# A two-layer DiT trunk on one core: the Fourier stage without GpSimd, x's squares summed by TensorE, fixed orders

## The chip, the cores and the metric

The kernel runs on one core of a Trainium2 chip. A core has five engines with instruction queues of their own: TensorE (PE, matmuls, with its weight loads as PEld), VectorE (DVE), ScalarE (ACT), GpSimd (POOL) and SyncE (SP, which issues most DMAs). The metric is the device time of one execution in microseconds.

## The reference, cut to what matters

Two layers over 512 tokens of width 1024. Layer 0 mixes by attention, layer 1 by a Fourier transform; each ends with a gated ConvFFN. The part that the change touches runs from the end of layer 0 to the start of layer 1's FFN:

```python
# end of layer 0
x = x + g2 * rms_norm(conv_ffn(h, ...), norm_g[0, 3])
# layer 1
h = modulate(rms_norm(x, norm_g[1, 0]), sh1, sc1)
y = fourier_mix(h) @ w_f                 # fft2 over (tokens, 256 channels of each of 4 groups), real part
x = x + g1 * rms_norm(y, norm_g[1, 1])
h = modulate(rms_norm(x, norm_g[1, 2]), sh2, sc2)
x = x + g2 * rms_norm(conv_ffn(h, ...), norm_g[1, 3])

def rms_norm(x, g):
    return x * lax.rsqrt(jnp.mean(x * x, axis=-1, keepdims=True) + EPS) * g
```

## The kernel before, in words

**Layout.** Activations are kept transposed: `xT` and `yT` are 128 partitions x 8 channel tiles x 512 tokens, in fp32. The tokens are worked in two halves of 256 (`halves`), so that one half's norms and updates run beside the other half's matmuls. Every matmul of size is done as three (`mm3`, lines 107 to 111), on a high and a low part of each operand. A high part is a cast on ACT, a low part a subtraction on DVE; `split` (line 130) issues both.

**What sets the order.** The program is written in one order, and a planner then places each engine's instructions by priority and by its own costs. `later(n)` shifts the priority (a negative number is earlier), `follow(i, j)` and `behind_pe` write an order between two instructions of one engine by hand, and `fence`/`held` keep some DVE and ACT work behind a point of the program. Parts that are to be interleaved are generators, advanced by `pump`.

**Norms.** The sum over channels is a matmul with ones: `stat_add` (line 195) adds a tile of squares in four matmuls with 32 output rows; `rstd` takes the reciprocal root (one ACT, four DVE operations); `spread` (line 227) brings the result to all partitions with one more matmul and copies it to SBUF as `Rs`. `YStat` squares y as its tiles are finished, adds most squares on POOL (line 303) and gives the last ones to PE directly.

**The last down sweep of layer 0** (`down_part`, `part`) makes y tile by tile, first for half 0, then for half 1. After half 0, `between` issues the update of x for half 0, `plain.tiles`, so that it runs beside half 1's matmuls: for each of eight tiles a DVE product of y, the gate `der` and `Rs`, a DVE add into `xT`, a high part `hst` on ACT and a low part `lst` on DVE of x times the layer's scale, a square on ACT, and an add of six of the eight squares on POOL (line 421) into `yT`'s tile 0.

**The Fourier stage.** `over_channels(g, h)` transforms the channels of group g for the two token tiles of half h into `Z` (half 0 scaled by its rms factor on the way out of PSUM; for half 1 the factor goes into the token tables, `tables(1, r1)`). `group(g, ts)` then sums over the token tiles `ts` with the cosine tables `ct` into `A` and with the sine tables `st` into `B`; `cosines(None, ...)` makes the Nyquist rows `N`. The rms factors are wanted with tokens on partitions, which `columns` (line 462) makes: four matmuls with the squares as stationary operand, and `rstd` on four columns. `shift` makes the transform of the constant shift. Half 1's update of x (`rest`) is pumped in between. The products with the weights (`wh`, `wl` of `w_f`) follow.

**Passages.** `joined` is the step from attention to layer 0's FFN: update of x, squares, sums, factor, and `remod`, which makes the FFN's operands `hh`, `hl` two tiles at a time or, for the tiles in `single`, one at a time. `joint` is the same step from the Fourier stage to layer 1's FFN, with two tiles per DVE product (`both` broadcasts the factor); its sums are advanced by `plain.runs`.

Of the kernel before, what the change touches and what calls it, by code (L numbers as in the profile page):

```python
# [85 lines left out]
def kernel(ctx: ExitStack, tc: tile.TileContext, a):  # L86
# [29 lines left out]


# [246 lines left out]
    def joined(ys, h, pps, nxt):  # L364
# [37 lines left out]
    class Plain:  # L402

        def __init__(self):
            self.acc = yT[:, 0, :]
            self.last = yT[:, KC - 1, :]

        def tiles(self, ys, h, l, gi, pps, am, eng=None):
            hs = halves[h]
            R = stat_bcast(ys.sums(pps, h), pps)  # L410
            yield
            for k in range(KC):
                x_update(h, l, gi, R, k, eng)
                x = xT[:, k, hs]
                S.activation(out=hst[:, k, hs], in_=x, func=AF.Copy, scale=am[:, k:k + 1])
                V.scalar_tensor_tensor(out=lst[:, k, hs], in0=x, scalar=am[:, k:k + 1], in1=f(hst[:, k, hs]),  # L416
                                       op0=ALU.mult, op1=ALU.subtract)
                sq = mk(cp, [P, T], F32, "sq", 2)[:, :HT] if 0 < k < KC - 1 else (self.last if k else self.acc)[:, hs]
                S.activation(out=sq, in_=x, func=AF.Square)
                if 0 < k < KC - 1:  # L420
                    G.tensor_tensor(out=self.acc[:, hs], in0=self.acc[:, hs], in1=sq, op=ALU.add)
                if k % 2:
                    yield


        def joint(self, ys, h, pps, am):
# [13 lines left out]
            for ks in ([[0], [1]] if h == 0 else [[0, 1]]) + [[2, 3], [4, 5], [6, 7]]:  # L440
# [3 lines left out]
                with later(0 if h else -10000):  # L444
                    V.tensor_tensor(out=t, in0=y, in1=both(R, n), op=ALU.mult)
                    i = V.tensor_tensor(out=x, in0=x, in1=t, op=ALU.add)
                    if h == 0 and ks == [1]:
                        self.mark = i
                    for k in ks:
                        S.activation(out=hh[:, k, hs], in_=xT[:, k, hs], func=AF.Copy, scale=am[:, k:k + 1])  # L450
                        V.scalar_tensor_tensor(out=hl[:, k, hs], in0=xT[:, k, hs], scalar=am[:, k:k + 1],
                                               in1=f(hh[:, k, hs]), op0=ALU.mult, op1=ALU.subtract)
                if ks[-1] % 2:
                    y = yT[:, ks[-1] - 1:ks[-1] + 1, hs]
                    S.activation(out=y, in_=xT[:, ks[-1] - 1:ks[-1] + 1, hs], func=AF.Square)
# [6 lines left out]
        def columns(self, h, pps):  # L462
            ps = mk(pps, [P, T], F32, "misc", 2)
            for i in range(2):
                t = 2 * h + i
                for n, s in enumerate((self.acc, self.last)):
                    PE.matmul(ps[:, 2 * i:2 * i + 2], lhsT=s[:, t * P:(t + 1) * P], rhs=ones32[:, :2], start=n == 0,
                              stop=n == 1)
            return rstd(ps[:, :4])
# [903 lines left out]
    def ffn(l, xp, ready, pre, mid, gem, plain=None):  # L1373
# [43 lines left out]
        def down_part(gi, w, g_, d, hs, ps=None, end=False):  # L1417
# [5 lines left out]
            if end:  # L1423
                ys.add(pps, yT[:, d, sl], hs)

# [116 lines left out]
        for gi, (f0, nch) in enumerate(GROUPS[l]):  # L1542
# [78 lines left out]
    def between(y):  # L1621
        fourier_early(2)
        pump(plain.tiles(y, 0, 0, 3, pps, n1[0], V), 6)
# [10 lines left out]
    with ExitStack() as es:  # L1634
# [15 lines left out]
        split(ft[0], ft[1], raw([P, 2, 256], a["dft_c"]), G)  # L1650
# [4 lines left out]
        def over_channels(g, h):  # L1655
            ps = mk(pps, [P, 2, 256], F32, *(("misc", 2) if h else ("mm", 6)))
            m = {}
            for i in range(2):
                ts_ = slice((2 * h + i) * P, (2 * h + i + 1) * P)
                for c in range(2):  # L1660
                    k = 2 * g + c
                    m[i, c] = mm3(ps[:, i, :], hst[:, k, ts_], lst[:, k, ts_], ft[0][:, c, :], ft[1][:, c, :],
                                  i + c == 0, i + c == 2)

            for c in range(2):
                follow(m[1, c][c], m[0, c][c])
# [3 lines left out]
            for t in range(2):  # L1670
                rc = r0[:, 2 * t:2 * t + 1]
                held(S.activation(out=Z[0][:, t, g, :], in_=ps[:, t, :], func=AF.Copy, scale=rc))
                held(V.scalar_tensor_tensor(out=Z[1][:, t, g, :], in0=ps[:, t, :], scalar=rc,
                                            in1=f(Z[0][:, t, g, :]), op0=ALU.mult, op1=ALU.subtract))


        def tables(h, r=None):
            if h == 0:
                for (th, tl), src in ((ct, lc), (st, ls)):
                    split(th[:, 0:2, :], tl[:, 0:2, :], src[:, 0:2, :], G)  # L1680
                return
            for i in range(2):
                t = 2 * h + i
                rc = r[:, 2 * i:2 * i + 1]
                for (th, tl), src in ((ct, lc), (st, ls)):
                    S.activation(out=th[:, t, :], in_=src[:, t, :], func=AF.Copy, scale=rc)
                    V.scalar_tensor_tensor(out=tl[:, t, :], in0=src[:, t, :], scalar=rc, in1=f(th[:, t, :]),
# [35 lines left out]
        def cosines(key, dst, lhs, ts, b):  # L1723
            ps = over_tokens(key, 0, lhs, ct, ts)
            if ts[-1] == TT - 1:
# [200 lines left out]
```

## Time and profile before

| | |
|---|---|
| runs of the kernel | 1110.02, 1112.4, 1114.91 us; median 1112.4 us |
| profiled execution | 1111.27 us, of which the span from first to last instruction is 1109.5 us |
| mean granted TensorE clock | 0.995 |
| busy: PE, DVE, ACT, POOL | 1082.2, 896.1, 595.7, 128.9 us |

Times in the profile count from the start of the span. A row of the timeline has the start, the duration, the engine, the line, the operation with output <- inputs, and the shapes; a bracket tells how long the engine was idle before it and who ended that. Neighbouring instructions of one kind are merged (xN). A plain fp32 matmul (the sums, the spread) leaves two records, each of the three of `mm3` one. A row of the stretches has the length and then, for each engine, the busy time and the number of instructions, the granted TensorE clock (1.00 is full speed), the DMA share and GB/s. A row of the waits has who waited for whom, the total in us, how often, and the longest. A row of the groups has the number of instructions, the busy us in all and the mean in ns.

### The profile page before, as it was taken

How to read it: one execution, taken by the hardware profiler on the slowest of the kernel's cores; microseconds unless marked ns; L12 is line 12 of the kernel's file. 1: busy time of each engine (PE TensorE's matmuls, PEld its weight loads, DVE VectorE, ACT ScalarE, POOL GpSimd, SP SyncE). 2: the span in 40 equal slices, each digit the busy share in tenths (PEclk: the TensorE clock that was granted, in tenths of full speed). 3: DMA queues.
4: the chain of work that ended last, by engine and by line, in shares of the span. 5: the costliest groups of instructions: out<-in, count | busy, mean ns of one | idle time of the engine just before them, and what ended most of it. 6: DMA issues, size and time to landing. Idle time of an engine off the chain costs nothing. (4 is left out here: it accounts for less than half of the span.)

```text
span 1109.5 us, 22276 instructions
## 1 busy us (share of the span) xinstructions
PE 1082.2 (98%) x9220; PEld 1013.0 (91%) x9220; DVE 896.1 (81%) x1457; ACT 595.7 (54%) x1047; POOL 128.9 (12%) x136
## 2 busy tenths in 40 slices
PE   9999999999999999999999998999999999999995
PEld 5699888869899999999999998989999999999995
DVE  5789877664689966879999878878997998979756
ACT  4452455665666633552465446768755654655542
POOL 0046123412100000000000133300000000000012
PEclk9999999999999999999999999999999999999998
DMA  9676100273231565327624600833206433332342
GB/s 368 273 256 209 39 18 22 76 292 126 77 153 42 173 242 204 115 86 263 245 77 164 232 35 21 281 100 134 77 30 196 147 109 115 105 105 86 105 148 77
DMA packets 33774, 156.01 MB, mean 141 GB/s; under 512 B 3460, under 2 KB 8196, under 8 KB 22024
## 3 DMA queue, kind: packets, MB, share of 16 engines
q1 hardware_dynamic: 32520, 150.39, 37.9%
q0 software_dynamic: 1152, 4.19, 1.5%
q8 instruction: 72, 1.18, 0.4%
q14 instruction: 30, 0.25, 0.1%
HBM read 148.28 MB, written 6.29 MB: 139 GB/s over the span
## 5 line engine op out<-in xcount | busy, mean ns | idle before, releaser
L131 ACT CAST wh<-raw 128x1024 fp32r<-128x1024 f32 (+2 forms) x207 | 190.7, 933 | 145.5 <-PE mm L109 102.0
L131 DVE TENSOR_TENSOR wl<-raw,wh 128x1024 fp32r<-128x1024 f32 (+2 forms) x205 | 219.9, 1079 | 60.4 <-ACT wh L131 57.8
L108 PE MATMUL mm<-hh,wh 128*128 128x256 f32 x856 | 240.7, 283 | 3.6 <-ACT sq L1335 1.9
L109 PE MATMUL mm<-hl,wh 128*128 128x256 f32 x856 | 238.0, 279 | 0.4 <-DVE hl L353 0.3
L110 PE MATMUL mm<-hh,wl 128*128 128x256 f32 x856 | 237.7, 278 | 0.5 <-DVE wl L131 0.5
L108 PEld LDWEIGHTS mm<-hh,wh 128*128 128x128 f32 x856 | 161.0, 189 | 9.8 <-ACT sq L1335 6.1
L109 PEld LDWEIGHTS mm<-hl,wh 128*128 128x128 f32 x856 | 161.2, 188 | 0.9 <-DVE hl L353 0.5
L110 PEld LDWEIGHTS mm<-hh,wl 128*128 128x128 f32 x856 | 160.8, 188 | 0.7 <-DVE wl L131 0.7
L108 PE MATMUL mm<-xh,wh 128*128 128x256 f32 x492 | 136.8, 279 | 0.0
L109 PE MATMUL mm<-xl,wh 128*128 128x256 f32 x492 | 136.7, 278 | 0.0
L110 PE MATMUL mm<-xh,wl 128*128 128x256 f32 x492 | 136.5, 278 | 0.0
L108 PE MATMUL mm<-zh,wh 128*128 128x256 f32 x384 | 109.4, 285 | 0.3
L109 PE MATMUL mm<-zl,wh 128*128 128x256 f32 x384 | 106.3, 277 | 0.0
L110 PE MATMUL mm<-zh,wl 128*128 128x256 f32 x384 | 106.3, 277 | 0.0
L108 PEld LDWEIGHTS mm<-xh,wh 128*128 128x128 f32 x492 | 92.3, 188 | 1.2 <-issue 0.8
L109 PEld LDWEIGHTS mm<-xl,wh 128*128 128x128 f32 x492 | 92.5, 188 | 0.6 <-issue 0.4
L110 PEld LDWEIGHTS mm<-xh,wl 128*128 128x128 f32 x492 | 92.5, 188 | 0.1
L108 PEld LDWEIGHTS mm<-zh,wh 128*128 128x128 f32 x384 | 72.1, 188 | 5.5 <-ACT sq L1338 4.7
L109 PEld LDWEIGHTS mm<-zl,wh 128*128 128x128 f32 x384 | 72.2, 188 | 0.0
L110 PEld LDWEIGHTS mm<-zh,wl 128*128 128x128 f32 x384 | 72.1, 188 | 0.0
L303 POOL TENSOR_TENSOR gacc<-gacc,sq 128x256 f32<-128x256 f32 (+1 forms) x23 | 20.4, 887 | 396.6 <-ACT sq L301 396.2
L1396 ACT ACTIVATE cv<-mm,cols 128x512 f32<-128x512 f32 x59 | 45.8, 779 | 12.1 <-PE mm L110 8.2
(457 smaller groups left out, 2794.8 us busy)
## 6 DMA issues: line engine op xcount, KB each, us to landing
raw<-in_w_up SPq DMA_DIRECT2D x42, 1024.0 KB, 4.9
xT<-in_mod_r SPq DMA_DIRECT2D x20, 1024.0 KB, 5.0
raw<-in_w_down SPq DMA_DIRECT2D x32, 384.0 KB, 3.1
raw<-in_mod_p SPq DMA_DIRECT2D x8, 1024.0 KB, 5.1
raw<-in_w_down SPq DMA_DIRECT2D x16, 512.0 KB, 4.5
raw<-in_w_in SPq DMA_DIRECT2D x6, 1024.0 KB, 8.0
yT<-in_mod_r SPq DMA_DIRECT2D x10, 512.0 KB, 6.8
raw<-in_w_out SPq DMA_DIRECT2D x4, 1024.0 KB, 5.8
```

The lines of the kernel that those rows point to most:

```text
L108: i = PE.matmul(out, lhsT=ah, rhs=bh, start=start, stop=False, skip_group_check=skip)
L109: PE.matmul(out, lhsT=ah, rhs=bl, start=False, stop=False, skip_group_check=skip)
L110: return i, PE.matmul(out, lhsT=al, rhs=bh, start=False, stop=stop, skip_group_check=skip)
L131: i = S.copy(out=h, in_=src), eng.tensor_tensor(out=l, in0=src, in1=f(h), op=ALU.subtract)
L303: G.tensor_tensor(out=self.acc[:, sl], in0=self.acc[:, sl], in1=sq[:, sl], op=ALU.add)
L1396: S.activation(out=cv, in_=ps, func=AF.Identity, bias=bc, scale=wc[1])
```

## The change

- `Plain.tiles` becomes `Plain.gated`. The gate is multiplied into y in the down sweep (one ACT operation per part); the update is done on pairs of tiles, product and add on DVE; the squares are written over y in pairs, and nothing is added on POOL. For half 1 the product of the first pair reads the factor from PSUM, and the DVE operations have a written order.
- `Plain.totals` sums all eight tiles of squares on PE with `stat_add` and takes `rstd`; `columns` then turns the result with two small matmuls and a copy. For half 0 both stand in the last down sweep (`first_norms`, behind the parts of tiles 6 and 7).
- The splits of `ft` and of the tables of half 0 move from POOL to DVE.
- PE's order in the Fourier stage is written out with `in_turn`: each matmul follows the one before it in the program. `shift` comes late, token tiles 2 and 3 are summed in two rounds over the groups, and the Nyquist sums come last.
- `joint` gets a written DVE order for half 0 and other priorities; `joined` makes the first two tiles of half 0 one at a time; `md(pair=True)` drops leftover half buffers.

The diff, cut to its core:

```diff
+    def in_turn(step, *args):
+        ops = nc.cur_bb.bb.instructions
+        at = len(ops)
+        r = step(*args)
+        for o in [o for o in ops[at:] if o.engine == mybir.EngineType.PE]:
+            if turn[0] is not None:
+                tc.add_manual_dep(o, turn[0], ...)
+            turn[0] = o.name
+        return r
...
     def md(pair=False):
-        if pair or not spare_md:
+        if pair:
+            spare_md.clear()
+        if not spare_md:
...
         for k in range(0, KC, 2):
             with later(-10000 if h else 0):
-                remod(h, *nxt, R, [k], (0, 4) if h else ())
+                remod(h, *nxt, R, [k], (0, 4) if h else (0,))
...
-        def tiles(self, ys, h, l, gi, pps, am, eng=None):
+        def gated(self, ys, h, pps, am):
             hs = halves[h]
-            R = stat_bcast(ys.sums(pps, h), pps)
+            r = rstd(ys.sums(pps, h)[:, :W4])
             yield
+            if h:
+                Rp, Rs = spread(r, pps, copy=False)
+                R = mk(cp, [P, HT], F32, "Rs", 3)
+                S.copy(out=R, in_=Rp)
+            else:
+                Rp = R = spread(r, pps)
+            yield
+            turn, low = [], []
+            for k in range(0, KC, 2):
+                x, y = (v[:, k:k + 2, hs] for v in (xT, yT))
+                t = md(True)
+                with later(-10000 if h else 0):
+                    turn.append(V.tensor_tensor(out=t, in0=y, in1=both(R if k else Rp), op=ALU.mult))
+                    turn.append(V.tensor_tensor(out=x, in0=x, in1=t, op=ALU.add))
+                    for c in (k, k + 1):
+                        S.activation(out=hst[:, c, hs], in_=xT[:, c, hs], func=AF.Copy, scale=am[:, c:c + 1])
+                        low.append(V.scalar_tensor_tensor(out=lst[:, c, hs], in0=xT[:, c, hs], ...))
+                    S.activation(out=y, in_=x, func=AF.Square)
+            if h:
+                turn = turn[:2] + low[:2] + turn[2:] + low[2:]
+                for n in range(1, len(turn)):
+                    follow(turn[n], turn[n - 1])
+
+        def totals(self, h, pps):
+            ps = mk(pps, [P, T], F32, "misc", 2)
             for k in range(KC):
...
-                if 0 < k < KC - 1:
-                    G.tensor_tensor(out=self.acc[:, hs], in0=self.acc[:, hs], in1=sq, op=ALU.add)
+                stat_add(ps, yT[:, k, halves[h]], HT, k == 0, k == KC - 1)
+            with later(-10000):
+                return rstd(ps[:, :W4])
...
         def joint(self, ys, h, pps, am):
...
+                    i = [update(ks) for ks in ([0], [1], [2, 3], [4, 5], [6, 7])]
+                turn = [*i[0], *i[1], line[0], line[1], *i[2]]
+                for n in (3, 4):
+                    turn += [line[2 * n - 4], line[2 * n - 3], *i[n]]
+                for n in range(1, len(turn)):
+                    follow(turn[n], turn[n - 1])
+                self.mark = i[2][1]
...
-        def columns(self, h, pps):
+        def columns(self, h, r, pps):
             ps = mk(pps, [P, T], F32, "misc", 2)
-            for i in range(2):
-                t = 2 * h + i
-                for n, s in enumerate((self.acc, self.last)):
-                    PE.matmul(ps[:, 2 * i:2 * i + 2], lhsT=s[:, t * P:(t + 1) * P], rhs=ones32[:, :2], ...)
-            return rstd(ps[:, :4])
+            for b in range(2):
+                PE.matmul(ps[64 * b:64 * b + 64, :2], lhsT=r, rhs=con[:, K_QD + b:K_QD + 4:2], start=True, stop=True)
+            c = mk(fx, [P, 2], F32, "rc%d" % h)
+            with later(-10000):
+                V.tensor_copy(out=c, in_=ps[:, :2])
+            return c
...
             if end:
                 ys.add(pps, yT[:, d, sl], hs)
+                if l == 0:
+                    S.activation(out=yT[:, d, sl], in_=yT[:, d, sl], func=AF.Copy, scale=der[:, 0, 3, d:d + 1])
...
                 for d in range(1, KC):
                     part(d, [1])
+                    if l == 0 and d > KC - 3:
+                        behind_pe(norms)
...
-        split(ft[0], ft[1], raw([P, 2, 256], a["dft_c"]), G)
+        split(ft[0], ft[1], raw([P, 2, 256], a["dft_c"]))
...
-            ps = mk(pps, [P, 2, 256], F32, *(("misc", 2) if h else ("mm", 6)))
+            ps = mk(pps, [P, 2, 256], F32, *(("misc", 2) if h and g != 2 else ("mm", 6)))
...
-                    split(th[:, 0:2, :], tl[:, 0:2, :], src[:, 0:2, :], G)
+                    split(th[:, 0:2, :], tl[:, 0:2, :], src[:, 0:2, :])
...
-        r0 = plain.columns(0, pps)
-        fb = shift()
+        fences.clear()
         tables(0)
-        nyh, nyl = wpair([4, D])
-        split(nyh, nyl, raw([4, D], a["w_ny"]))
-        rest = plain.tiles(ys, 1, 0, 3, pps, n1[0], V)
-        pump(rest)
-        over_channels(0, 0)
-        fence()
-        over_channels(3, 0)
-        pump(rest)
...
+        rest = plain.gated(ys, 1, pps, n1[0])
+        in_turn(over_channels, 0, 0)
+        in_turn(pump, rest)
+        for g in (1, 2):
+            in_turn(over_channels, g, 0)
+        in_turn(pump, rest)
+        pump(rest)
+        in_turn(over_channels, 3, 0)
+        in_turn(group, 0, [0, 1])
+        in_turn(over_channels, 0, 1)
+        for g in (1, 2):
+            in_turn(group, g, [0, 1])
+        v1 = in_turn(plain.totals, 1, pps)
+        for g in (1, 2):
+            in_turn(over_channels, g, 1)
+        nyh, nyl = wpair([4, D])
+        split(nyh, nyl, raw([4, D], a["w_ny"]))
+        r1 = in_turn(plain.columns, 1, v1, pps)
+        tables(1, r1)
+        in_turn(over_channels, 3, 1)
+        in_turn(group, 3, [0, 1])
+        fb = in_turn(shift)
+        for g in (2, 0, 1, 3):
+            in_turn(group, g, [2])
         fence()
+        for g in (2, 0, 1, 3):
+            in_turn(group, g, [3])
+        in_turn(cosines, None, N, [z[:, :, :, P] for z in Z], list(range(TT)), True)
```

More of the change, by code (lines that the diff above doesn't have):

```diff
@@ L115, in follow @@
             mybir.DependencyClass.NoSync, mybir.DependencyReason.DATA), reason="order")
+    turn = [None]
+    def in_turn(step, *args):
[4 more added lines that the diff above has]
+            if turn[0] is not None:
+                tc.add_manual_dep(o, turn[0], mybir.DependencyInfo(
+                    mybir.DependencyClass.NoSync, mybir.DependencyReason.DATA), reason="order")
+            turn[0] = o.name
+        return r
     fences = {}
@@ L439, in joint, with update @@
             yield
-            for ks in ([[0], [1]] if h == 0 else [[0, 1]]) + [[2, 3], [4, 5], [6, 7]]:
+            line = {}
+            def update(ks):
                 n = len(ks)
@@ L443, in joint @@
                 t = md(True)[:, :n, :]
[L444 to L452, printed above, removed]
+                i = V.tensor_tensor(out=t, in0=y, in1=both(R, n), op=ALU.mult)
+                j = V.tensor_tensor(out=x, in0=x, in1=t, op=ALU.add)
+                for k in ks:
+                    S.activation(out=hh[:, k, hs], in_=xT[:, k, hs], func=AF.Copy, scale=am[:, k:k + 1])
+                    line[k] = V.scalar_tensor_tensor(out=hl[:, k, hs], in0=xT[:, k, hs], scalar=am[:, k:k + 1],
+                                                     in1=f(hh[:, k, hs]), op0=ALU.mult, op1=ALU.subtract)
                 if ks[-1] % 2:
                     y = yT[:, ks[-1] - 1:ks[-1] + 1, hs]
-                    S.activation(out=y, in_=xT[:, ks[-1] - 1:ks[-1] + 1, hs], func=AF.Square)
+                    with later(0 if h else 10000):
+                        S.activation(out=y, in_=xT[:, ks[-1] - 1:ks[-1] + 1, hs], func=AF.Square)
+                return i, j
+            if h:
+                for k in range(0, KC, 2):
+                    update([k, k + 1])
+            else:
+                with later(-10000):
[6 more added lines that the diff above has]
+                self.mark = i[2][1]
             yield
@@ L1622, in between, with first_norms @@
         fourier_early(2)
-        pump(plain.tiles(y, 0, 0, 3, pps, n1[0], V), 6)
+        pump(plain.gated(y, 0, pps, n1[0]), 10)
+    def first_norms():
+        r = plain.totals(0, pps)
+        yield
+        rc.append(plain.columns(0, r, pps))
+    rc = []
+    norms = first_norms()
     with ExitStack() as es:
@@ L1661, in over_channels @@
                     k = 2 * g + c
[L1662 to L1666, printed above, removed]
+                    mm3(ps[:, i, :], hst[:, k, ts_], lst[:, k, ts_], ft[0][:, c, :], ft[1][:, c, :],
+                        i + c == 0, i + c == 2)
             if h:
@@ L1670, in over_channels @@
             for t in range(2):
[L1671 to L1674, printed above, removed]
+                r = rc[0][:, t:t + 1]
+                S.activation(out=Z[0][:, t, g, :], in_=ps[:, t, :], func=AF.Copy, scale=r)
+                V.scalar_tensor_tensor(out=Z[1][:, t, g, :], in0=ps[:, t, :], scalar=r,
+                                       in1=f(Z[0][:, t, g, :]), op0=ALU.mult, op1=ALU.subtract)
         def tables(h, r=None):
```

49 lines of the change are left out of this document (9 added, 40 removed).

## The prediction

> **What bounds the kernel now.** I read the page first, then the busy time by stretches around the Fourier stage, the waits of the whole run, and the timelines of that stage.
>
> ```profile
> span 1109.5 us, 22276 instructions
> ...
> PE 1082.2 (98%) x9220; PEld 1013.0 (91%) x9220; DVE 896.1 (81%) x1457; ACT 595.7 (54%) x1047; POOL 128.9 (12%) x136
> ```
>
> TensorE (PE) is busy for 1082.2 of 1109.5 us. Anything that takes work from another engine pays only where PE waits for that engine. So the size of the prize is the time that PE loses in the stage that is edited:
>
> ```profile
> core 0: us, PE busy (x) PEld busy (x) DVE busy (x) ACT busy (x) POOL busy (x), PEclk, DMA share, GB/s
> 651.70:665.90 14.20, 14.20 (x122) 14.20 (x121) 14.17 (x26) 7.60 (x20) 8.82 (x9) 1.00 0.01 2
> 665.90:676.70 10.80, 10.23 (x104) 9.57 (x103) 8.43 (x24) 6.54 (x17) 3.97 (x5) 0.84 0.17 51
> 676.70:692.70 16.00, 13.73 (x106) 12.56 (x104) 14.39 (x34) 9.56 (x25) 5.54 (x6) 1.00 0.01 2
> ```
>
> From 651.70 to 665.90 the last down sweep runs on PE without a gap, although VectorE (DVE) is full (14.17 of 14.20): what the first half's update costs there is hidden. From 665.90 on PE has gaps (13.73 of 16.00) and once a lowered clock (0.84). The waits say for whom:
>
> ```profile
> PE misc L467 <- POOL yT L421: 1.2, 1, 1.2
> ...
> PE mm L108 <- ACT hh L352: 1.1, 1, 1.1
> ...
> PE misc L110 <- DVE hl L416: 0.7, 1, 0.7
> ...
> PE misc L198 <- POOL cv L303: 0.6, 1, 0.6
> ```
>
> Two of the four are GpSimd (POOL) adds that carry squares, one is the second half's update on DVE. The fourth (L352) lies elsewhere, at the start of the first FFN, in the helper `remod`, which the change also touches. The stage on PE's timeline:
>
> ```profile
> 665.89 0.97 PE L467 MATMUL misc<-ones,yT 128*128 128x2 f32 x8
> 666.72 0.25 PE L108 MATMUL misc<-sh,wh 128*128 128x4 f32 x1
> 667.55 0.36 PE L108 MATMUL mm<-wh,hh 128*128 128x256 f32 x1
> ...
> 668.95 1.13 PE L198 MATMUL misc<-cv,ones 128*32 128x64 f32 x32 [0.57 <-POOL cv L303]
> ...
> 690.12 1.05 PE L467 MATMUL misc<-ones,yT 128*128 128x2 f32 x8 [1.18 <-POOL yT L421]
> 691.04 0.36 PE L108 MATMUL misc<-wh,hh 128*128 128x256 f32 x1
> ...
> 697.17 0.28 PE L108 MATMUL mm<-ct,Z 128*4 128x258 f32 x1
> ...
> 699.99 0.28 PE L108 MATMUL mm<-B,wh 128*128 128x256 f32 x1
> ```
>
> The last down part ends at 665.89 and the first product with `B` starts at 699.99: 34.10 us. This is the stretch that I recompute.
>
> **The change part by part.**
>
> *Work on PE in that stretch.* Between the rows 697.17 and 699.99 stand exactly 24 matmuls: 2.82 / 24 = 0.1175 us each. `over_channels` issues 96 (4 groups, 4 token tiles, 2 halves of channels, 3 each), `group` 96, the Nyquist sums 12: 204 x 0.1175 = 23.97 us, the same before and after. `shift` stays, 667.55 - 666.72 = 0.83 us, only later. The new `totals` sums eight tiles of squares with `stat_add`. Four such sums, in another place, stand in this pair:
>
> ```profile
> 309.46 0.72 PE L198 MATMUL misc<-yT,ones 128*32 128x64 f32 x32
> ...
> 310.12 0.38 PE L108 MATMUL mm<-hh,wh 128*128 128x256 f32 x1
> ```
>
> 0.66 us for 32 records, so 1.32 for the 64 of one `totals`, with some 0.1 to get back to wide matmuls 1.4. There are two: 2.8 us added. The second half's norm of y (four sums, 32 records) stays, 0.76. The old `columns`, 666.72 - 665.89 = 0.83 and 691.04 - 690.12 = 0.92, go. The new `columns` is two matmuls onto 64 rows with two columns, four records. The trace does not show it: no less than four L198 records (0.08), no more than the old one (0.83); I take 0.3, nearer the small end since it has half the records and half the width. The spread of the second half's factor:
>
> ```profile
> 674.46 0.60 PE L234 MATMUL misc<-Rs,con 128*128 128x256 f32 x2
> ...
> 675.02 0.28 PE L108 MATMUL mm<-wh,hh 128*128 128x256 f32 x1
> ```
>
> 0.56 less the one matmul between, 0.44, as before. Sum after: 23.97 + 0.83 + 2.8 + 0.76 + 2 x 0.3 + 0.44 = 29.4 us against 34.10. Without any wait the stage would gain 4.7 us, although PE gets 2.8 + 0.6 - 1.75 = 1.65 us more work.
>
> *Where it must wait.* The PE order is now written out (`in_turn`), so PE cannot step past a late operand. Behind the second half's spread stand `over_channels(3, 0)`, group 0, `over_channels(0, 1)`, groups 1 and 2, 60 matmuls, 7.05 us, then `totals(1)`, whose last pair of squares is wanted 0.99 later: 8.0 us after the spread. What DVE and ACT need until then goes by these rows, pair products of the later passage among them, which have the new update's form:
>
> ```profile
> 746.73 0.69 DVE L445 TENSOR_TENSOR md_t<-yT,Rs 128x512 f32<-128x512 f32 x1
> 747.45 0.69 DVE L446 TENSOR_TENSOR xT<-xT,md_t 128x512 f32<-128x512 f32 x1
> ```
>
> ```profile
> 655.43 0.47 DVE L416 SCALAR_TENSOR_TENSOR hl<-xT,der,hh 128x256 fp32r<-128x256 f32 x1
> 655.83 0.95 DVE L328 SCALAR_TENSOR_TENSOR md_t<-yT,der,Rs 128x256 f32<-128x256 f32 x1
> ...
> 655.67 1.70 POOL L421 TENSOR_TENSOR yT<-yT,sq 128x256 f32<-128x256 f32 x2 [1.92 <-ACT sq L419]
> ```
>
> ```profile
> L416 DVE SCALAR_TENSOR_TENSOR hl<-xT,der,hh 128x256 fp32r<-128x256 f32 x16 | 9.4, 595 | 0.0
> ...
> L1673 DVE SCALAR_TENSOR_TENSOR Z<-mm,st_v,Z 128x256 fp32r<-128x256 f32 x8 | 3.6, 476 | 0.0
> ```
>
> The second fence shows why GpSimd matters beyond its own adds: the DVE operation that starts beside a POOL add takes 0.95 instead of 0.47 us, and the mean of the 16 low parts is 595 ns. Without those adds I use 0.40 from start to start (655.43 to 655.83) for a single and 0.72 for each of a dependent pair. First pair 1.44; ACT's copy about 0.57 (used for two `Z` splits); two low parts 0.8; three more pairs 4.3; two further `Z` splits 0.8: 7.9 us. Then ACT still has two copies or the square, 0.6 to 1.4: 8.5 to 9.3 against 8.0. So PE waits 0.5 to 1.3 us here. With changes between wide and narrow matmuls and a `Z` split that comes late I book 1.6 (ends 0.2 and 9, see the rivals). The stage: -4.7 + 1.6 = **-3.1 us**.
>
> *What is behind it.* After `totals(1)` the chain of the reciprocal root and the new `columns` has `over_channels(1, 1)` and `(2, 1)` as cover, 24 x 0.1175 = 2.8 us. That chain up to a spread was, elsewhere,
>
> ```profile
> 730.45 0.31 ACT L204 ACTIVATE st_r<-misc,con 128x64 f32<-128x64 f32 x1 [0.39 <-PE misc L198]
> ...
> 732.28 0.67 PE L234 MATMUL misc<-Rs,con 128*128 128x256 f32 x2
> ```
>
> 1.83 us with a product that is not needed here. The tables (four ACT, four DVE operations of about 0.5, two of each ahead of the next user) are covered by `over_channels(3, 1)`, group 3 and `shift`, 24 matmuls and 0.83, 3.65 us. Nothing is booked. If DVE is late by more than 1 us there, this cover is gone one for one.
>
> *First half.* Its totals now stand ahead of down part 7. The cover is the sweep, 14.2 us, in which DVE needs 8 pair operations (5.8) and 8 low parts (3.2), about 9 us, beside the sweep's adds. Nothing is booked for waiting; the 1.4 is in the sum. Folding the gate into the down sweep adds an ACT operation of about 0.5 us per part (the L342 row below has that width) on an engine that is busy for 7.60 of 14.20. The splits of `ft` and the tables go from POOL to DVE, three of the width of a pair product (0.69), under the same sweep or the first matmuls. POOL keeps the adds of `YStat` (L303); they no longer queue behind L421, so the wait of 0.57 goes. The small load of `w_ny` and its split move behind `over_channels(2, 1)`; nothing reads them before the products at the end, and no earlier reader waits behind that load on SP's queue.
>
> *Start of the first FFN.* `joined` now makes the first two tiles of the first half one by one:
>
> ```profile
> 293.73 2.50 DVE L348 TENSOR_TENSOR yT<-xT,Rs 128x512 f32<-128x512 f32 x4 [1.20 <-ACT Rs L237]
> ...
> 295.69 0.32 PE L198 MATMUL misc<-gacc,ones 128*32 128x64 f32 x8
> 296.44 1.12 ACT L352 CAST hh<-yT 128x512 fp32r<-128x512 f32 x2
> ...
> 297.10 0.72 PE L108 MATMUL mm<-hh,wh 128*128 128x256 f32 x4 [1.09 <-ACT hh L352]
> ```
>
> ```profile
> 315.33 0.49 DVE L341 SCALAR_TENSOR_TENSOR yT<-xT,der,Rs 128x256 f32<-128x256 f32 x1 [1.74 <-ACT Rs L237]
> ...
> 315.86 0.51 ACT L342 ACTIVATE hh<-yT,mods 128x256 fp32r<-128x256 f32 x1 [0.56 <-DVE yT L341]
> ```
>
> The second half already does it so: 315.33 to 316.37 for the first tile, 1.04 us. From 293.73 that is 294.8, before PE comes at 295.9. The wait of 1.09 goes: **-1.1 us**. Late next is the second pair: the later of the two copies in the 296.44 row ended at 297.56, and it is wanted 36 matmuls on, near 300.2. Two ACT operations to restore y are put last, on an idle ACT.
>
> *Passage to the second FFN (`joint`).* The first wait is unchanged:
>
> ```profile
> 734.46 0.40 PE L1456 MATMUL mm<-hh,xh 128*128 128x258 f32 x1 [0.53 <-ACT hh L450]
> ```
>
> since first product, first add, first copy are the same. The written order puts the low part of tile 1 ahead of the next pair, and DVE then waits for an ACT copy (0.51 by the L342 row) that the next pair used to fill: between 0 and 0.5 us of new waiting, I take **+0.2**. `md`, the fences and the PSUM pool of one group: no row moves for them, 0 +-0.2.
>
> Sum: -3.1 - 1.1 + 0.2 = **-4.0 us**. Against the profiled execution (1111.27 us with a span of 1109.5) that is 1107.3; the median shown is 1112.4, 1.1 above it, so the forecast is 1112.4 - 4.0 = **1108.4 us**, -0.36%. About 0.5% (5.6 us) is what a measurement here can tell from no change, so this counts as the same.
>
> **The rivals.**
>
> *The written order leaves no wait.* -4.7 - 1.1 = -5.8: 1106.6 us, just beyond the bound. For it: the list's cover is only 0.5 us short at the low end. Against it: every estimate of DVE is without latency between engines.
>
> *The low clock stays.* In the stretch of narrow matmuls and the 0.57 us wait from 665.89 on PE was put at half clock:
>
> ```profile
> 669.00:673.00 4.00, 4.00 (x47) 3.59 (x48) 3.15 (x8) 2.04 (x6) 1.21 (x1) 0.57 0.37 108
> ```
>
> Four microseconds at a mean clock of 0.57 are 4 x 0.43 = 1.7 us lost. The new stage has less of such work together before its wide matmuls, so I booked the low clock as gone, but the wait with `totals(1)` behind it, 1.3 + 1.4 = 2.7 us, is nearly as long as the 3.1 from 665.89 to 668.95. If it drops there: -4.0 + 1.7 = -2.3, 1110.1 us. The Trainium skill, "TensorE: Matmul & The Clock Gate", section "Part 1: The HAM clock gate (the "warmup" mystery)", says that the clock is halved after at least one idle window of about 3.4 us. By that rule alone no wait of 0.57 us could have done it, and the trace, where it was halved, disagrees unless narrow matmuls count as idle; with a rule of pure idleness my removed drop would have no reason, and the sum would be the 1110.1 of this rival.
>
> *The splits of `Z` queue behind the update.* The second half's update has priority over the `Z` splits on DVE, and PE is held to its list. If all of the update goes first (1.44 + 0.6 + 0.8 + 4.3 + 2.4 for six low parts = 9.5 us after the spread) and then two splits (0.8), group 1, wanted 36 matmuls or 4.2 us after the spread, starts 6 us late, with the low clock after it. -4.7 + 6 + 1.7 - 1.1 + 0.2 = +2.1: 1114.5 us, slower. It decides from a wait of 5.6 us on (4.7 + 0.9). For it: the priorities; against it: DVE has room for `Z` of group 1 before the spread lands.
>
> *Nothing to see.* The waits come back one after another in the same size, and only the FFN's start is left: -1, 1111.4 us.
>
> **How the numbers follow.** Forecast 0.45, own range 1106.8 to 1110.0; no wait 0.22; low clock 0.12; `Z` late 0.11; nothing to see 0.10. The range 1104.5 to 1113.5 takes in the no-wait case with 2 us of spread of the runs below it, and the rest up to a part of the slow rival. Faster by over 0.5% (below 1106.8): most of the no-wait case and some of the forecast, 0.27. Slower by over 0.5% (above 1118) needs the `Z` rival and a further wait behind it: 0.08. Same: 0.65.
>
> **What would show it.** Right: from the end of the last down part to the first `B` product about 29.6 us (34.1 less 3.1, less the 1.4 that now stands ahead of that part); no L421 on POOL; low parts of the second half at a mean of 0.48; no wait for L352 near 296; the first part of the second FFN as before. Wrong: waits of PE for `Z` splits or for the last squares of over 3 us, a stretch at clock 0.50 after `totals(1)`, or gaps in the last down sweep before part 7 because the first half's squares are late.

## The result, and the profile after

The changed kernel takes 1121.95 us in the median (1121.68 to 1123.04) beside 1112.38 us for the kernel before: 1.0086 times as long, with a 95% interval of 1.0070 to 1.0101. Forecast were 1108.4 us and a range of 1104.5 to 1113.5. The time is outside the range and on the other side of no change. The profiled execution took 1121.68 us with a span of 1119.9, 10.4 us more than the span before.

The totals of the page after:

```profile
span 1119.9 us, 22480 instructions
...
PE 1095.8 (98%) x9340; PEld 1027.0 (92%) x9340; DVE 886.0 (79%) x1448; ACT 601.3 (54%) x1055; POOL 113.6 (10%) x121
```

VectorE and GpSimd have less to do, as intended (896.1 to 886.0, 128.9 to 113.6). TensorE is busy for 13.6 us more. The 120 added records are cheap ones, so something else became slower. Cutting the run at five places of the PE timeline shows where:

| stretch | before, us | after, us | difference |
|---|---|---|---|
| start of the span to the first product of the first FFN | 297.10 | 296.33 | -0.8 |
| from there to the end of the last down part | 368.8 | 376.0 | +7.2, of which 1.1 are the first half's totals, moved there |
| Fourier stage, to the first `B` product | 34.1 | 31.9 | -2.2 |
| first `B` product to the first product of the second FFN | 34.5 | 35.1 | +0.7 |
| from there to the end of the span | 375.0 | 380.5 | +5.5 |

The stage that was edited became shorter. The loss lies in the two FFNs, whose matmuls the change does not touch: 6.1 + 5.5 = 11.6 us. The middle of the first FFN, 260 us with no gap worth the name, first before and then after (columns as in the table of stretches above; the first number in brackets is the count of matmuls):

```profile
330.00:590.00 260.00, 258.88 (x2221) 253.19 (x2220) 222.95 (x272) 129.32 (x192) 0.00 (x0) 1.00 0.44 158
```

```profile
330.00:590.00 260.00, 259.65 (x2183) 254.32 (x2182) 218.77 (x266) 126.12 (x188) 0.00 (x0) 1.00 0.44 158
```

In equal time, at a granted clock of 1.00, with the same DMA load and PE a little busier, 38 matmuls fewer get done: 1.7%. So each matmul is slower. The groups of the page, before and after (the last numbers of a row ahead of the second bar are the busy time and the mean ns of one):

```profile
L109 PE MATMUL mm<-hl,wh 128*128 128x256 f32 x856 | 238.0, 279 | 0.4 <-DVE hl L353 0.3
...
L109 PE MATMUL mm<-xl,wh 128*128 128x256 f32 x492 | 136.7, 278 | 0.0
...
L109 PE MATMUL mm<-zl,wh 128*128 128x256 f32 x384 | 106.3, 277 | 0.0
```

```profile
L109 PE MATMUL mm<-hl,wh 128*128 128x256 f32 x856 | 238.1, 279 | 0.1
...
L109 PE MATMUL mm<-xl,wh 128*128 128x256 f32 x492 | 139.4, 284 | 0.0
...
L109 PE MATMUL mm<-zl,wh 128*128 128x256 f32 x384 | 107.9, 281 | 0.0
```

Products that read `hl` are unchanged (279 ns). Those that read `xl` and `zl` have become longer by 6 and 4 ns. A record is longer than its share of PE's time because matmuls overlap, so the start times say it better. Two steps of one sweep, 34 matmuls apart in each kernel, before and after:

```profile
646.44 0.28 PE L108 MATMUL mm<-xh,wh 128*128 128x256 f32 x1
...
650.29 0.28 PE L109 MATMUL mm<-xl,wh 128*128 128x256 f32 x1
```

```profile
651.26 0.28 PE L108 MATMUL mm<-xh,wh 128*128 128x256 f32 x1
...
655.33 0.28 PE L109 MATMUL mm<-xl,wh 128*128 128x256 f32 x1
```

3.85 / 34 = 0.113 us from start to start before, 4.07 / 34 = 0.120 after. Over the whole trace, products of `xh`, `xl` with `wh`, `wl` went from 114.2 to 119.7 ns, those of `zh`, `zl` from 114.1 to 119.0, those of `hh`, `hl` stayed (115.3 and 115.1). There are 3 x 492 and 3 x 384 of the first two kinds: 1476 x 5.5 + 1152 x 4.9 ns = 13.8 us, enough for all of the loss.

What `xh`, `xl`, `zh`, `zl` have in common is that they moved in SBUF. The change allocates two new 8-byte tiles, `rc0` and `rc1`, in the pool `fx`, which lies ahead of the FFN's operands. Each takes a slot of 32 bytes. In the built programs `xh` starts at byte 153344 of each partition before and 153408 after, `zh` at 196352 and 196416; `wh` (112192), `wl` (132672), `hh` (37120) and `hl` (53760) are where they were. Everything below tests whether these 64 bytes are the cause.

### The profile page after: what moved, and what is told of

Its sections match the earlier page's. It is cut to its first block, busy times and chain, and to the rows that moved or that the text cites. A ratio compares the mean times of both kernels' runs of the same rounds, so it can differ in the third digit from the quotient of the medians.

```text
span 1119.9 us, 22480 instructions
## 1 busy us (share of the span) xinstructions
PE 1095.8 (98%) x9340; PEld 1027.0 (92%) x9340; DVE 886.0 (79%) x1448; ACT 601.3 (54%) x1055; POOL 113.6 (10%) x121
## 3 DMA queue, kind: packets, MB, share of 16 engines
q0 software_dynamic: 1152, 4.19, 1.5%
## 4 chain that ended last, share of the span: by engine, by line
PE 82%; DVE 10%; ACT 5%; DMA 1%; issue 1%; POOL 0%; POOLq 0%; DVEq 0%; SPq 0%; ACTq 0%
PE mm L108 24%; PE mm L109 22%; PE mm L110 22%; DVE wl L144 2%; PE PT L1107 1%; ACT wh L144 1%; PE gm L108 1%; ACT yT L365 1%; PE O L109 1%; PE gm L109 1%; PE gm L110 1%; PE O L108 1%; PE O L110 1%; PE S L108 1%; PE S L110 1%
## 5 line engine op out<-in xcount | busy, mean ns | idle before, releaser
L144 DVE TENSOR_TENSOR wl<-raw,wh 128x1024 fp32r<-128x1024 f32 (+2 forms) x207 | 221.7, 1077 | 66.7 <-ACT wh L144 66.3
L144 ACT CAST wh<-raw 128x1024 fp32r<-128x1024 f32 (+2 forms) x207 | 190.7, 932 | 154.4 <-PE mm L109 113.7
L108 PE MATMUL mm<-xh,wh 128*128 128x256 f32 x492 | 139.7, 285 | 0.0
L109 PE MATMUL mm<-xl,wh 128*128 128x256 f32 x492 | 139.4, 284 | 0.0
L110 PE MATMUL mm<-xh,wl 128*128 128x256 f32 x492 | 139.4, 283 | 0.0
```

Of the source, the lines that this page charges most:

```text
L108: i = PE.matmul(out, lhsT=ah, rhs=bh, start=start, stop=False, skip_group_check=skip)
L109: PE.matmul(out, lhsT=ah, rhs=bl, start=False, stop=False, skip_group_check=skip)
L110: return i, PE.matmul(out, lhsT=al, rhs=bh, start=False, stop=stop, skip_group_check=skip)
L144: i = S.copy(out=h, in_=src), eng.tensor_tensor(out=l, in0=src, in1=f(h), op=ALU.subtract)
```

## The experiments

Each ratio below is to runs of the kernel before taken in the same series (medians 1112.03, 1111.30 and 1110.92 us), with its 95% interval in brackets.

### Placement

**The kernel before with 64 unused bytes in that pool, and the changed kernel with 64 more.**

```diff
+    mk(fx, [P, 16], F32, "fxpad")      # behind the opening of pool fx
```

> The kernel before, with nothing of the change, but with the same 64 unused bytes per partition in front of the pool of the FFN operands. Placement theory: it alone makes the kernel slower by 13 to 15 us (1450 matmuls by 5.5 ns, 1100 by 4.8, 450 by 2.8, 300 by 2.3 = 15.2), 1125 to 1128 us. Rival: the time stays at 1112 us.

> The changed kernel with 64 unused bytes per partition added in front of the pool of the FFN operands, so that the tiles xh, xl, zh, zl, Z and ct, which the two new 32-byte tiles rc0 and rc1 had moved by 64 bytes, lie 128 bytes from their old place. Placement theory (a matmul is slower when its two operands start in the same half of a 128-byte line): matmuls of xh and xl with wh, wl go back from 119.7 to 114.2 ns from start to start, those of zh, zl from 119 to 114, some 13 us in all, and the kernel ends near 1109 us, about 3 us under the kernel before. Rival (the written orders and the extra sums cost the 10 us, the pace is a symptom of something else in the program): the time stays at 1120 to 1122 us.

Measured: before_pad64 1124.58 us, 1.0114 (1.0092 to 1.0137) times the kernel before; after_pad64 1118.65 us, 1.0061 (1.0042 to 1.0079). The same stretch and groups of before_pad64:

```profile
330.00:590.00 260.00, 259.65 (x2183) 254.34 (x2182) 219.02 (x267) 126.34 (x187) 0.00 (x0) 1.00 0.43 155
```

```profile
L109 PE MATMUL mm<-xl,wh 128*128 128x256 f32 x492 | 139.6, 284 | 0.0
```

2183 matmuls, to the piece as in the changed kernel, and 284 ns. No instruction differs from the kernel before, only addresses. So placement by itself makes the whole loss and more: this kernel hasn't the change's gains, and its Fourier stage, itself shifted, ran into longer stretches of low clock (37.4 us instead of 34.1, with a clock of 0.50 from 677 to 681 us). What fell is my first idea of the rule, that the operands must start on the right half of a 128-byte line: after_pad64 has them 128 bytes off and should have been back at about 1109 us. It recovered about a quarter, 3.3 of 13 us.

**128 bytes in the kernel before.** The same edit with `[P, 32]`.

> The kernel before with 128 unused bytes per partition in that place. If the half of the 128-byte line decides, nothing changes: 1112 us, 114.2 ns. If any move of these tiles away from the old place costs (another bank, another distance), it is slower as with 64 bytes, 1125 us or more.

Measured: 1120.03 us, 1.0070 (1.0048 to 1.0092). A miss for the 128-byte rule again: products of `xh` run at 117.2 ns, between the 114.2 and the 119.8 of the other placements.

That led to another reading of the traces. While a matmul streams its moving operand, the stationary operand of the *next* matmul is loaded: in the trace of before this load starts 3 ns behind the matmul (median) and takes 188 ns. For every pair of neighbouring 256-column matmuls that start less than 135 ns apart I took the difference of these two addresses, modulo 256 bytes, and the mean time from start to start (count in brackets):

```
difference        0             32            64            96            128           160          192           224
before            119.1 (177)                 119.4 (19)                  119.8 (8)                  114.6 (6620)
after             119.3 (2719)                119.3 (23)                  118.5 (369)                115.1 (3723)
before_pad64      119.3 (2722)                                            118.7 (374)                115.1 (3689)
before_pad128     119.2 (173)                 117.2 (2932)                                           115.0 (3706)
after_pad64                                   117.2 (2924)                                           115.1 (3722)
```

Before, nearly all pairs stood at 192, and that is the quick place. The change brought 2719 of them to 0.

Which stationary operand counts, the next one or the matmul's own, these traces leave open: in all but some 30 to 90 of about 6950 pairs of a build both give the same difference. The period does come out of them: taken modulo 512, pairs at 192 and at 448 run alike (114.5 and 114.8 ns over thirteen of the traces), while 64 and 192 differ, so it is 256 bytes and not 128.

**A test of the difference.** If it is the difference that counts and not the place of `xh` alone, then moving `wh`, `wl` *and* `xh` to `zl` together by 64 bytes must leave the products of `xh` quick and slow down those of `hh`, `hl`, which stay in place.

```diff
-WPAD = 8
+WPAD = 24
```

> The kernel before with 64 more bytes of padding in front of wh and wl: these and all that lie behind them (xh, xl, zh, zl, Z, ct) move by 64 bytes, hh and hl stay. If the difference of the two operands' addresses decides, matmuls of xh, xl, zh, zl with wh, wl keep 114 ns (the difference stays 192), and those of hh, hl with wh, wl go from 115 to 119 or 120 (192 becomes 128): 2550 of them by 5 ns and 450 with weights in xh, some 13 to 15 us, 1125 to 1128 us. If the absolute place of xh and zh decides, these go to 119.8 as with the 64 bytes behind wh, and hh, hl keep 115.

Measured: 1125.90 us, 1.0129 (1.0115 to 1.0143). The groups:

```profile
L109 PE MATMUL mm<-hl,wh 128*128 128x256 f32 x856 | 240.8, 282 | 0.0
...
L109 PE MATMUL mm<-xl,wh 128*128 128x256 f32 x492 | 136.7, 278 | 0.0
```

`xl`, which moved, is back at 278; `hl`, which did not move, goes from 279 to 282. From start to start: 114.1 and 118.8 ns; 3248 pairs at a difference of 128 run at 118.8. The rule of the difference holds, and a theory by the address of one operand doesn't.

**Two finer steps** (one profiled execution each), with `[P, 8]` and `[P, 24]` in place of `[P, 16]`:

> The kernel before with 32 unused bytes in front of the FFN operand pool: the difference of the two addresses for xh, xl, zh, zl with wh, wl becomes 224 modulo 256 instead of 192. With differences of 0, 64, 128 and 192 at 119.5, 117.5, 119.5 and 114.3 ns, a value that only counts in steps of 64 bytes leaves 114.3; one that falls off smoothly gives about 117.

> The same with 96 bytes: the difference becomes 32 modulo 256. Counted in steps of 64 bytes, it is as for 0 with 64 bytes of padding, 119.5 ns; if it falls off smoothly, about 118.5.

Measured: 1125.97 and 1118.44 us. At a difference of 224 118.2 ns (2548 pairs), 160 119.1 (366), 32 116.9 (2546), 96 119.9 (370). A value that counts in steps of 64 bytes would have given 114.3 at 224 and 119.5 at 32, so that is refuted; a smooth fall (117 and 118.5) misses by 1.2 and 1.6 ns. The curve over the difference is not a plain one: 119 at 0, 117 at 32 and 64, 120 at 96, 119 at 128 and 160, 114 to 116 at 192, 118 at 224.

**The change at the old addresses.** The two tiles are laid into `wpad`, 32 bytes ahead of `wh` that the kernel had unused, so that every operand of the FFN stands where it was.

```diff
-            mk(wp, [P, WPAD], F32, "wpad")
+            rc_at.append(mk(wp, [P, WPAD], F32, "wpad"))
...
-            c = mk(fx, [P, 2], F32, "rc%d" % h)
+            c = rc_at[0][:, 4 * h:4 * h + 2]
```

> The changed kernel with rc0 and rc1 laid into unused padding that stood in front of wh, so that every tile lies where it lay in the kernel before. Theory after the runs with padding (the start-to-start time of a matmul depends on the address of its moving operand less that of the stationary operand loaded next, modulo 256 bytes: 192 gives 114 ns, 64 gives 117 to 118, 0 and 128 give 119 to 120): nearly all matmuls are back at 192, 114 ns, and the time is that of the kernel before less what the change itself gains. At equal placement (both 128 bytes off) the change was 1.4 us under the kernel before, from which 1109 to 1111 us. Rival: the placement hid a gain or loss of the change of its own; then it is under 1107 or over 1113.

Measured: 1109.05 us, 0.9975 (0.9963 to 0.9986) times the kernel before. The stretch and a group:

```profile
330.00:590.00 260.00, 258.92 (x2229) 253.23 (x2229) 223.94 (x274) 130.31 (x194) 0.00 (x0) 1.00 0.44 158
```

```profile
L109 PE MATMUL mm<-xl,wh 128*128 128x256 f32 x492 | 136.4, 277 | 0.0
```

46 matmuls more than after, in equal time, and 277 ns. Some 6700 pairs stand at a difference of 192 again and run at 114.5 ns. What the change was made for gains 0.25%, 2.8 us; 64 bytes cost 1.0086 - 0.9975 = 1.1%, 12 us.

### The parts of the change

**The start of the first FFN alone**, in the kernel before:

```diff
-                remod(h, *nxt, R, [k], (0, 4) if h else ())
+                remod(h, *nxt, R, [k], (0, 4) if h else (0,))
```

> The kernel before with one edit of the change: in joined, the first two tiles of the first half are made one at a time. By the forecast the wait of 1.1 us for L352 near 296 us goes and the kernel gains 1.1 us, 1111.3. Rival: the wait moves to the next pair or to the start of the second half (now 0.3 us at 320), and the gain is 0 to 0.3 us.

Measured: 1110.61 us, 0.9990 (0.9977 to 1.0003). The interval reaches no change, but the rows of the timeline are clear:

```profile
293.29 0.70 PE L234 MATMUL misc<-Rs,con 128*128 128x256 f32 x2 [0.21 <-DVE Rs L229]
...
296.30 0.28 PE L108 MATMUL mm<-hh,wh 128*128 128x256 f32 x1
```

From the spread of the factor to the first FFN product 3.01 us, without a wait; in the kernel before, where the product starts at 297.10, 4.51 us:

```profile
292.59 0.70 PE L234 MATMUL misc<-Rs,con 128*128 128x256 f32 x2 [0.21 <-DVE Rs L229]
```

**The old passage to the second FFN**, in the change at the old addresses (`joint` as in the kernel before):

> Restored placement, with the passage to the second FFN (joint) as in the kernel before. In the profiles at equal placement that passage took 0.85 us longer with the new order, mostly since the second half's sums came in four pieces instead of one. Theory: 0.5 to 0.9 us are gained against the kernel with restored placement. Rival (later work takes it up): no difference.

Measured: 1117.61 us, 1.0053 (1.0040 to 1.0065), some 8.6 us more than with the new passage. I had expected a small gain. New waits, and a low clock behind them:

```profile
732.10 0.39 PE L1488 MATMUL mm<-hh,xh 128*128 128x258 f32 x1 [0.74 <-ACT hh L480]
...
735.08 1.16 PE L1492 MATMUL mm<-hl,xh 128*128 128x258 f32 x4 [1.74 <-DVE hl L481]
...
756.05 0.66 PE L213 MATMUL mm<-yT,ones 128*32 128x64 f32 x16 [3.05 <-ACT yT L485]
```

```profile
735.00:742.00 7.00, 6.92 (x56) 6.69 (x57) 6.30 (x12) 4.74 (x9) 0.00 (x0) 0.76 0.01 2
...
756.00:764.00 8.00, 7.95 (x91) 6.77 (x92) 5.82 (x14) 5.17 (x12) 0.00 (x0) 0.59 0.61 258
```

The waits are 5.5 us, of which 0.5 stood there before; the clock takes 7 x 0.24 + 8 x 0.41 = 5.0 more. From the first product of the second FFN to the end the run takes 384.4 us, after_place 375.2. The new order in `joint` isn't a refinement at +0.2 us: together with the other parts the old one costs 8.6 us. DVE's rows show why for the first two waits:

```profile
731.75 1.28 DVE L475 TENSOR_TENSOR md_t<-yT,misc 128x512 f32<-128x512 f32 x2
732.95 0.68 DVE L476 TENSOR_TENSOR xT<-xT,md_t 128x512 f32<-128x512 f32 x1
733.55 0.48 DVE L481 SCALAR_TENSOR_TENSOR hl<-xT,der,hh 128x256 fp32r<-128x256 f32 x1
733.95 0.68 DVE L476 TENSOR_TENSOR xT<-xT,md_t 128x512 f32<-128x512 f32 x1
734.55 0.48 DVE L481 SCALAR_TENSOR_TENSOR hl<-xT,der,hh 128x256 fp32r<-128x256 f32 x1
```

Without the written order the products and adds of two later pairs go ahead of the two low parts that PE stands waiting for. The third wait, of 3.05 us, has another source:

```profile
752.29 0.70 PE L249 MATMUL misc<-Rs,con 128*128 128x256 f32 x2
...
753.43 1.29 DVE L475 TENSOR_TENSOR md_t<-yT,Rs 128x512 f32<-128x512 f32 x2 [0.29 <-ACT Rs L252]
```

PE makes the spread of the second half's factor only at 752.29; in the kernel before, with the same `joint`, it stood at 737.49. DVE, idle for 10.8 us until 752.23, can start that half's products only behind it, and the squares that PE sums at 756.05 come late. Which of the other edits moved the low parts and the spread was not traced.

**Priority for the second half's factor of y.** The largest wait left in the changed stage (below) is for `Rs`. Its operations are issued earlier:

```diff
-            r = rstd(ys.sums(pps, h)[:, :W4])
+            ps = ys.sums(pps, h)
+            with later(-10000 if h else 0):
+                r = rstd(ps[:, :W4])
...
+                with later(-10000):        # half 1: spread and its copy
```

> The same with one more edit: the reciprocal root, the spread and the copy of the second half's factor get the high priority (later(-10000)) that the update behind them has. In the changed kernel PE waited 1.65 us for that Rs, since DVE and ACT had put Z and ct splits ahead of it. Theory (that wait is a matter of order): it goes, and the kernel gains 1 to 1.6 us on the one with restored placement. Rival: DVE is full in that stretch; the splits are late instead, PE waits for Z or for the last squares (0.9 and 0.32 us now) in the same measure, and nothing is gained.

Measured: 1106.54 us, 0.9956 (0.9944 to 0.9969). The rows show the wait for `Rs` gone:

```profile
667.21 0.65 PE L213 MATMUL misc<-cv,ones 128*32 128x64 f32 x32
...
670.72 0.60 PE L249 MATMUL misc<-Rs,con 128*128 128x256 f32 x2
...
681.60 0.43 PE L213 MATMUL misc<-yT,ones 128*32 128x64 f32 x16 [0.89 <-ACT yT L446]
```

The waits for the squares stay (0.34 and 0.89), and one of 0.36 us for a high part of x is new. The stage takes 30.7 us instead of the 32.0 of after_place: 1.3 us, as expected. The medians differ by 2.5 us; the two intervals overlap slightly, and what the medians show beyond the 1.3 us was not traced.

**Squares ahead of the copies**, on top of it, for half 1 from the second pair on:

```diff
+                    if h and k:
+                        S.activation(out=y, in_=x, func=AF.Square)
                     for c in (k, k + 1):
...
-                    S.activation(out=y, in_=x, func=AF.Square)
+                    if not (h and k):
+                        S.activation(out=y, in_=x, func=AF.Square)
```

> Restored placement and the priority for the second half's factor (1106.5 us), and in the second half's update the square of a pair is issued ahead of its two copies from the second pair on. PE waited 0.89 and 0.34 us for these squares. Theory: 0.8 to 1.0 us are gained. Rival: the copies and the low parts behind them are late in turn, PE waits for the operands of the transform by as much, and nothing is gained.

Measured: 1106.05 us, 0.9960 (0.9948 to 0.9972): not to be told from place_prio. In the profile the stage goes from 30.7 to 29.9 us and the wait for the last squares from 0.34 + 0.89 to 0.70.

**The written order of PE left out**, in the change at the old addresses (`in_turn` no longer adds its order):

```diff
-            if turn[0] is not None:
-                tc.add_manual_dep(o, turn[0], ...)
```

> Restored placement, with PE's written order in the Fourier stage taken out (in_turn advances the steps but adds no order; the planner places the matmuls by its own costs). In the kernel with restored placement the written order leaves waits of 1.65, 0.34, 0.90 and 0.51 us. If the written order is what costs the forecast gain, the planner fills these and the stage gets 1 to 3 us shorter. If the order is worth something, the stage gets longer, as in the kernel before with its four waits and its many switches: 1 to 3 us slower than with the order.

Measured: 1106.73 us, 0.9965 (0.9953 to 0.9976). The planner's own order is no worse than the written one; the stage takes 30.5 us instead of 32.0, and PE waits twice in it, 0.42 us for the last squares and 0.47 ahead of the second `columns`:

```profile
681.02 0.43 PE L210 MATMUL misc<-yT,ones 128*32 128x64 f32 x16 [0.42 <-ACT yT L440]
...
685.00 0.28 PE L506 MATMUL misc<-con,st_v 128*64 128x2 f32 x4 [0.47 <-DVE st_v L220]
```

The intervals of the two versions overlap, so a loss by the written order is likely rather than shown; a gain by it of 1 to 3 us is ruled out. The order was not taken out of place_prio, so what it is worth beside the early factor is open.

place_prio, place_prio_sq and place_freeorder all beat both the kernel before, by 0.35 to 0.44%, and the changed one, by 1.2 to 1.3% (0.9956 / 1.0086 for place_prio).

## Why the prediction was wrong, point by point

**The step that failed.** "`md`, the fences and the PSUM pool of one group: no row moves for them, 0 +-0.2" priced the edits with no work in them at nothing, and the new tiles `rc0` and `rc1` weren't even in that list. They bring no instruction beyond two copies of 0.16 us, but as allocations they moved the FFN's four operand tiles by 64 bytes, and that cost 12 us, three times the whole forecast gain. No rival had it, because all of them looked at the edited parts and took the pace of every other matmul as given. The trace of before hardly gives the price: 6620 of 6824 pairs stand at one difference there. It did hold 204 others at 119 to 120 ns, for whoever set them beside the addresses in the built program.

**The sum without that step.** -4.0 us was forecast, -2.8 was measured at the old addresses, by its interval -1.6 to -4.1. The sign and the verdict "the same" would have been right. The three terms below, read from rows of the changed kernel, add to -1.1 - 1.5 + 0.7 = -1.9, inside that interval. The one profiled execution at the old addresses doesn't settle the rest: at 1110.96 us it lies near the upper end of its runs (1106.4 to 1112.12), with the clock at 0.57 from 122 to 126 us, where the traces of before and after show 1.00. One rival was also summed wrongly: the case without a wait leaves out the +0.2 of the passage; with it, it is -5.6 and 1106.8 us, on the bound instead of beyond it. By its terms:

*Stage: -3.1 forecast, -1.1 measured* (31.9 plus the 1.1 of the moved totals, against 34.1). The PE work was right. 64 records of `totals` were booked at 1.32, the new `columns` at 0.3 us:

```profile
668.36 1.10 PE L211 MATMUL misc<-yT,ones 128*32 128x64 f32 x64
669.38 0.39 PE L108 MATMUL mm<-xh,wh 128*128 128x256 f32 x1
...
672.46 0.28 PE L507 MATMUL misc<-con,st_v 128*64 128x2 f32 x4
672.67 0.39 PE L108 MATMUL mm<-wh,hh 128*128 128x256 f32 x1
...
674.25 0.65 PE L211 MATMUL misc<-cv,ones 128*32 128x64 f32 x32
...
679.58 0.67 PE L247 MATMUL misc<-Rs,con 128*128 128x256 f32 x2 [1.65 <-DVE Rs L242]
...
688.47 0.43 PE L211 MATMUL misc<-yT,ones 128*32 128x64 f32 x16 [0.32 <-ACT yT L441]
...
689.80 0.43 PE L211 MATMUL misc<-yT,ones 128*32 128x64 f32 x16 [0.90 <-ACT yT L441]
```

1.02 and 0.21. The wait for the last squares, forecast at 0.5 to 1.3, is 0.32 + 0.90 = 1.22. What was not foreseen is the 1.65 at 679.58, ahead of the update instead of in it. The spread was booked "as before", without asking what DVE does between the sums (674.25) and `Rs`:

```profile
675.56 0.70 DVE L144 TENSOR_TENSOR ct<-raw,ct 128x516 fp32r<-128x516 f32 x1 [0.82 <-ACT ct L144]
676.18 0.48 DVE L1723 SCALAR_TENSOR_TENSOR Z<-mm,rc,Z 128x256 fp32r<-128x256 f32 x1
676.57 0.21 DVE L218 TENSOR_SCALAR st_v<-misc 128x64 f32<-128x64 f32 x1
...
677.07 0.87 DVE L1723 SCALAR_TENSOR_TENSOR Z<-mm,rc,Z 128x256 fp32r<-128x256 f32 x2
...
679.02 0.41 DVE L242 TENSOR_TENSOR Rs<-st_v,con 128x256 f32<-128x256 f32 x1
...
688.20 2.46 DVE L439 SCALAR_TENSOR_TENSOR hl<-xT,der,hh 128x256 fp32r<-128x256 f32 x6
```

The table split that was moved from GpSimd to DVE and five splits of `Z` stand between the small operations of the root; from sums to spread it takes 5.33 us, in place_prio 3.51. My rival had the splits of `Z` queue behind the update; it came the other way round, the update's factor queued behind the splits. Waits of 1.65 + 1.22 where 1.6 was booked are the larger part of the 2.0 us missing; the other 0.7 was not traced. The low parts were right: (2.46 - 0.48) / 5 = 0.40 us from start to start, as used, and no L421 on GpSimd.

*The low clock*, booked as gone, is gone in the changed stage:

```profile
672.40:704.20 31.80, 28.94 (x324) 27.23 (x323) 25.77 (x62) 19.55 (x44) 0.00 (x0) 1.00 0.21 69
```

A wait of 1.65 us did not lower it, while in place_oldjoint 0.74 and 1.74 us a short burst apart were followed by a mean of 0.76. The Trainium skill, "TensorE: Matmul & The Clock Gate", section "Part 1: The HAM clock gate (the "warmup" mystery)", has the clock halved after at least one idle window of about 3.4 us; the first of these agrees with it, the second does not.

*Start of the first FFN: -1.1 forecast*, -1.5 by the rows (spread at 293.28, first product at 296.33, 3.05 us instead of 4.51), and before_joined has the same by itself. The table's -0.8 is less because the spread itself came 0.7 us later. In before_joined it is as late, and there the lag already stands at the sums at 281 us (281.52 beside 280.84), ahead of the edited rows.

*Passage: +0.2 forecast, +0.7 measured.* The first wait, "unchanged", is (0.53). New is a wait of 0.23 at the `B` products:

```profile
705.43 0.38 PE L109 MATMUL mm<-B,wh 128*128 128x256 f32 x1 [0.23 <-DVE mm L1777]
...
739.36 0.39 PE L1500 MATMUL mm<-hh,xh 128*128 128x258 f32 x1 [0.53 <-ACT hh L477]
```

The product that waits is the first to read the low part of `B` for groups 2 and 3. The row names an add on DVE, but that low part ends at 705.38,

```profile
704.70 0.68 DVE L144 TENSOR_TENSOR B<-mm,B 128x512 fp32r<-128x512 f32 x1
```

and in place_prio_sq the same wait of 0.22 is put down to it (L144). The new order brings the last of these sums to the end of the stage, right ahead of the products, and the prediction named nothing that would hide their splits. The rest of the 0.7 I didn't trace. What the +0.2 was booked for lies behind this stretch and costs nothing: DVE does wait for an ACT copy (0.18 us at 740.13), but PE doesn't wait for DVE there, and from the first product of the second FFN to the end after_place takes 375.2 us beside 375.0 before.

## What to carry to other kernels

When matmuls of a stage that wasn't edited get slower at full clock, compare the addresses of their operands before anything else, and try the change with every old tile at its old address: new tiles belong behind, or in padding, not ahead of operands in use. In a prediction an allocation is an edit with a price; ask what it moves, and let the range show that the price isn't known. And where work goes to an engine that had room on average, read that engine's queue between a sum and the operation that waits for its result: there a few splits of 0.5 us made a wait of 1.65 us that nobody had booked.

## What the runs showed of the hardware that I had not expected

The time from start to start of these 256-column matmuls depends on the difference, modulo 256 bytes, of the address of the streamed operand and that of the stationary operand loaded meanwhile (or its own, which nearly always gives the same difference): 114 to 116 ns at 192, 117 to 120 elsewhere. Six builds with the same instructions at other addresses (the kernel before and its five pads) lie between 1111 and 1126 us; part of that is low clock, which comes on top of the pace (in before_pad64 3.3 us more for the Fourier stage, with a clock of 0.50 in it).

What stays open: why 192 is best, which of the two stationary operands counts, and what in the memory or in the load of the stationary operand makes the steps; whether a difference not tried (in steps under 32 bytes) is better still; and an unevenness of about 2 ns within one difference (`hh` products between 113.8 and 115.8 ns at 192), of which one profiled execution per build can't tell whether it goes with the build or with the execution. The table is read from traces by order of the records, and only pairs under 135 ns are in it. That address differences decide is shown by before_wpad64 and after_place; the mechanism is not.
